# A 2-layer hybrid decoder step on one core: row products of the RWKV-7 chunk inverse moved to GpSimd, output weights split once and kept, group norm centred by a matmul

## The chip, the cores and the metric

One Trainium2 chip, one NeuronCore of it. TensorE (PE in the rows), VectorE (DVE), ScalarE (ACT) and GpSimd (POOL) each run their own instruction stream in order; SyncE (SP) only issues DMAs, also in order. The metric is the device time of one launch in microseconds, the median over runs.

## The reference, cut to what matters

Layer 0 (retention and RG-LRU) and both ConvFFNs are not touched. Layer 1 mixes time with RWKV-7: per head a 64x64 state, a per-head group norm of the result, and an output product.

```python
def rwkv7_step(S, inp):
    r_t, w_t, k_t, v_t, a_t, b_t = inp
    sa = jnp.einsum('bhij,bhj->bhi', S, a_t)
    S = S * w_t[:, :, None, :] + sa[..., None] * b_t[:, :, None, :] + v_t[..., None] * k_t[:, :, None, :]
    y = jnp.einsum('bhij,bhj->bhi', S, r_t)
    return S, y
...
    s_new, ys = lax.scan(rwkv7_step, s0, ...)          # 1040 prompt tokens, 16 heads of 64
    mu = jnp.mean(ys, axis=-1, keepdims=True)
    var = jnp.mean(jnp.square(ys - mu), axis=-1, keepdims=True)
    o = ((ys - mu) * lax.rsqrt(var + GN_EPS_C)).reshape(B, T, D) * p['gn_g'] + p['gn_b']
    bonus = jnp.sum(rh * kh * p['r_k'], axis=-1, keepdims=True) * vh
    o = (o + bonus.reshape(B, T, D)) * g
    return o @ p['w_o'], ...
```

All data are float32. The large products are done in three float32r passes: a weight block and its input are each split into a high and a low part.

## The kernel before, in words

The program runs layer 0, its FFN, Layer1A (all of RWKV-7 up to the recurrence; results go to scratch in DRAM), Layer1B (the recurrence and most of the output product), `finish` (the last quarter of the output product), and the second FFN. Instructions are emitted in the order in which they are to run: no scheduler reorders them.

**Layer1B.** The 1040 tokens are cut into 17 chunks of 64; a chunk's 16 heads are two halves, so there are 34 units (chunk, half). The string `UNIT = "pa z pt g1 u r r o r p2 g2 o o s o r y p3"` (L1641) is the order of work in one unit: `pa pt p2 p3` prepare the next unit (scores, transposes, the inverse's lower block), `z u s y` are the chain through the state, `g1 g2` the group norm of the previous unit, `r` takes one step of the inverse from a list, `o` one quarter of an output tile. So each unit has four `r` and four `o`. `s` ends with a copy of the new state on GpSimd (`s0v`, L1812), which stands once per unit in the trace and is used below as the unit's clock.

**The inverse (`inv_steps`, L1422).** For a group of four chunks, 128 blocks of 32x32 lie one per partition and I - A is inverted by forward substitution: row t takes a product of t x t elements (L1439, tile `pr`) and a sum over its rows (L1441, into column t of `mt`), both on VectorE; row t+1 reads column t. `CUTS` (L1636) puts rows 1 to 13 into three steps and each row from 14 to 31 into a step of its own. The first group is inverted in Layer1A; the other four (the last holds one chunk, on 32 partitions) in the recurrence, starting in units 0, 8, 16 and 24 and each to be done by the end of the sixth unit, when its results are loaded again from scratch. The block's input `at` is loaded in the first `r` of the same unit.

**Weights.** `load_next` (L270) loads blocks of 128x1024 (512 KB) two ahead on SP into two `wst` buffers. `split_next` (L279) makes `wh` on ScalarE and `wl` on VectorE (L323, L324), one block ahead, in two buffers each. The output weights `w_o`, eight blocks, are used four times, once for each block of about 260 tokens (`OBLK`), and loaded and split each time. The first three token blocks go beside the recurrence in the `o` slots, one output tile per unit in units 9 to 32; the last is `finish`.

**Group norm.** `gn_unit` (L1836): a matmul with the block of ones gives the sums (L1845), VectorE subtracts the mean (L1846), ScalarE squares (L1848). `gn_unit2`: a second matmul gives the variance (L1856), then ScalarE and VectorE make its inverse root (L1349 to L1352), and VectorE multiplies it in and applies the two gains (L1357, L1860, L1861); ScalarE and VectorE split the result (`yh`, `yl`).

Of the kernel before, what the change touches and what calls it, by code (L numbers as in the profile page):

```python
# [8 lines left out]
F32 = mybir.dt.float32  # L9
F32R = mybir.dt.float32r  # L10
AF = mybir.ActivationFunctionType
# [18 lines left out]
# ---------------------------------------------------------------- vectors  # L30
# [14 lines left out]
def constants():  # L45
    """Tables that depend on shapes alone."""
# [23 lines left out]
    m = np.zeros((128, 536), f)  # L70
# [9 lines left out]
    m[:, 408:536] = np.kron(np.eye(2), np.ones((64, 64)))  # L80
    c["masks"] = m
# [6 lines left out]
# ---------------------------------------------------------------- host layout  # L88
def cols(v):
    """(..., n*128) -> (128, ..., n): features on partitions."""  # L90
    v = np.asarray(v)
    r = v.reshape(v.shape[:-1] + (v.shape[-1] // 128, 128))
    return np.moveaxis(r, -1, 0)


def wblocks(w):
    """(K, M) -> (M/128, 128, K/128 * 128): one block per 128 output features."""
    k, m = w.shape
    return w.reshape(k // 128, 128, m // 128, 128).transpose(2, 1, 0, 3).reshape(m // 128, 128, k)


def gblocks(w, groups):
    """(K, 1024) cut along K in groups of g tiles -> blocks that hold 8, 4 or 2 output tiles x g K-tiles."""
# [89 lines left out]
# where the parts of a head pair's arithmetic stand beside the next products, in sixths of a 128-wide output tile  # L193
# [23 lines left out]
class Weave:  # L217
    """Emits dense steps and, between them, side steps as their share of the time comes up."""
# [43 lines left out]
class Prog:  # L262
# [6 lines left out]
    # ---- weights: loads two blocks ahead, exact split into two float32r parts one block ahead  # L269
    def load_next(self):  # L270
        if self.wq:
            w = self.wq.pop(0)
            src, pre = w if isinstance(w, tuple) else (w, None)
            n = src.shape[-1]
# [4 lines left out]
    def split_next(self):  # L279
        t, n, pre = self.loaded.pop(0)  # L280
        h = self.wsp.tile([128, 1024], F32R, tag="wh", name="wh")[:, :n]
        l = self.wsp.tile([128, 1024], F32R, tag="wl", name="wl")[:, :n]
        if pre is not None:
            self.scale_w(t, *pre)
        self.split(t, h, l)
        self.load_next()
        self.ready.append((h, l))
# [15 lines left out]
    def scale_w(self, t, kind, j):  # L303
        """Scales a block of w1 | a1 (or g1) by mix (j = 0) or 1 - mix along K."""
# [21 lines left out]
    # ---- one PSUM bank of a product: sum over k of W[k]^T X[k], in three exact float32r passes  # L326
# [21 lines left out]
    # steps of one 128-wide output tile, each token block in so many parts; evac(tb, psum view, c0, c1).  # L348
    # late: the weights of the next tile are not split before this one; pre: they are once its products are out
# [18 lines left out]
    # two tiles side by side at the start of a phase, each token block as soon as its norm is there  # L368
# [6 lines left out]
    # the same tile with the K-tiles outermost: each K-tile of X is done with as early as can be  # L375
# [15 lines left out]
    # steps of x += W^T y over a group of g K-tiles; a weight block holds 8/g output tiles  # L391
# [23 lines left out]
    # ---- RMS norm in parts: squares as the tiles of x become final, the scale per token block, then h  # L415
# [6 lines left out]
    # adds up squares over the features, all but the last few queued  # L422
# [8 lines left out]
    def rsqrt(self, y, v, t):  # L431
        """y = v ** -0.5: table value and one Newton step; t is scratch like v."""
# [17 lines left out]
    # emit(m, tb, rs) may return its second half, which then follows the next one's first  # L450
# [14 lines left out]
    # called after each step of the product that completes x: adds up the squares and queues the norm  # L465
# [36 lines left out]
class Layer0:  # L502
# [10 lines left out]
    # ---- retention, head h: q and k with the rotary applied (features on partitions), v by tokens  # L513
# [41 lines left out]
    def dense_ga(self, h, e):  # L555
        """Gate columns of head h: y = silu(g) * (normed o * gain), split as it comes."""
# [74 lines left out]
        # chunk 0: the sample rows, each with its own state, and the 16 leading prompt rows  # L631
# [68 lines left out]
        # the stages of a chunk are one step apart  # L700
# [8 lines left out]
    # ---- RG-LRU, one block of 128 features  # L709
# [21 lines left out]
    def lru_steps(self, g):  # L731
        """a = exp(-y) with y = 8 softplus(-lam) r, and sqrt(1 - a^2) = sqrt(t) (1 + a) with t = tanh(y / 2)."""
# [148 lines left out]
def softplus_neg(p, nc, pool):  # L881
    """lamc = 4 softplus(-lam) = 4 (max(-lam, 0) + ln(1 + exp(-|lam|)))."""
# [13 lines left out]
def layer0(p, pool, H, wv):  # L896
# [3 lines left out]
    # norm of the input: the squares of a token block beside the norm of the one before  # L900
# [25 lines left out]
    # the tensor engine's clock only rises with use  # L926
# [34 lines left out]
class FFN:  # L961
    """x += W_down^T (gelu(conv(W_ug^T h)) * (W_uv^T h)); f tiles are used in groups of four."""
# [1122 lines left out]
```

## Time and profile before

| what | value |
|---|---|
| runs (3) | 3524.53, 3528.8, 3534.92 us; median 3528.8 |
| profiled execution, first to last instruction | 3527.9 us |
| PE busy, DVE busy, ACT busy, POOL busy | 94%, 51%, 35%, 10% of the span |
| recurrence (units 0 to 33) | about 2218 to 2690 us of the span |
| `finish` and the norm after it | about 2690 to 2760 us |

No own time of the profiled execution stands beside its span, so sums are made against 3527.9 us; the median of the runs is 0.9 us above it. Busy shares over the whole span say little of the recurrence, which is 13% of it and has limits of its own: it is read by units and by windows.

### The profile page before, as it was taken

What the parts mean: (1) busy time and instruction counts of PE and PEld (TensorE: products, weight loads), DVE (VectorE), ACT (ScalarE), POOL (GpSimd) and SP (SyncE); (2) the same over time, 40 slices, a digit from 0 to 9 for tenths busy, and PEclk for the clock granted to TensorE, in tenths of its full rate; (3) what the DMA queues carried; (4) which work ended last, traced back from release to release, by engine and by line L of the source; (5) the groups of instructions that cost most, each with busy time, mean ns of one, the idle gap of its engine ahead of it and who ended that gap; (6) DMA issues with size and microseconds to landing.
All of it is one profiled execution on the core that took longest, in us unless ns stands there. A gap on an engine that the chain in (4) does not pass through costs nothing.

```text
span 3527.9 us, 55814 instructions
## 1 busy us (share of the span) xinstructions
PE 3305.9 (94%) x23480; PEld 3123.5 (89%) x23480; DVE 1800.3 (51%) x2860; ACT 1241.4 (35%) x2214; POOL 361.6 (10%) x650
## 2 busy tenths in 40 slices
PE   8999999998999999998978978788889999999998
PEld 7999999997999999997978878566767999999997
DVE  4444445556433333334765658677885533333334
ACT  4222224555322212123674444344445312212122
POOL 0110110000000000000111236111210000000000
PEclk9999999999999999999999989678999999999999
DMA  4111211111111111111356768845543111111111
GB/s 134 62 56 60 74 40 46 46 47 34 42 43 48 48 48 42 42 53 48 118 169 169 176 172 232 219 119 143 152 129 96 37 49 46 45 49 42 48 48 64
DMA packets 303066, 294.33 MB, mean 83 GB/s; under 512 B 233056, under 2 KB 248704, under 8 KB 300640
## 3 DMA queue, kind: packets, MB, share of 16 engines
q1 hardware_dynamic: 294368, 262.95, 25.6%
q0 software_dynamic: 8448, 27.82, 2.5%
q8 instruction: 185, 3.03, 0.4%
q14 instruction: 65, 0.53, 0.1%
HBM read 218.95 MB, written 67.47 MB: 81 GB/s over the span
## 4 chain that ended last, share of the span: by engine, by line
PE 29%; DVE 12%; DMA 4%; ACT 3%; issue 3%; SPq 1%; POOL 1%; DVEq 0%; POOLq 0%; ACTq 0%
PE d L337 8%; PE d L335 8%; PE d L336 8%; DVE pr L1439 2%; DVE mt L1441 1%; PE hs L1325 1%; DVE xsl L324 1%; DMA x<-d_pp 1%; DVE wl L324 1%; DMA kq<-d_kq 1%; PE nrm L429 1%; DMA at<-d_ab 1%; DVE x L1213 1%; DVE T L1439 0%; ACT x L1188 0%
## 5 line engine op out<-in xcount | busy, mean ns | idle before, releaser
L335 PE MATMUL d<-xsh,wh 128*128 128x350 f32 (+1 forms) x3656 | 1207.6, 330 | 11.5 <-ACT xsh L323 7.7
L337 PE MATMUL d<-xsl,wh 128*128 128x350 f32 (+1 forms) x3656 | 1193.6, 326 | 5.2 <-DVE xsl L324 5.1
L336 PE MATMUL d<-xsh,wl 128*128 128x350 f32 (+1 forms) x3656 | 1188.0, 325 | 4.4 <-DVE wl L324 4.4
L335 PEld LDWEIGHTS d<-xsh,wh 128*128 128x128 f32 x3656 | 696.2, 190 | 23.2 <-ACT xsh L323 9.3
L337 PEld LDWEIGHTS d<-xsl,wh 128*128 128x128 f32 x3656 | 694.6, 190 | 16.0 <-DVE xsl L324 14.7
L336 PEld LDWEIGHTS d<-xsh,wl 128*128 128x128 f32 x3656 | 696.9, 191 | 7.1 <-DVE wl L324 5.2
L335 PE MATMUL d<-T,wh 128*128 128x350 f32 (+1 forms) x1380 | 463.7, 336 | 15.8 <-DVE x L405 8.9
L324 DVE TENSOR_TENSOR wl<-wst,wh 128x1024 fp32r<-128x1024 f32 x248 | 303.1, 1223 | 320.3 <-ACT wh L323 320.3
L336 PE MATMUL d<-T,wl 128*128 128x350 f32 (+1 forms) x1380 | 445.2, 323 | 2.5 <-DVE wl L324 2.5
L337 PE MATMUL d<-T,wh 128*128 128x350 f32 (+1 forms) x1380 | 445.3, 323 | 1.4 <-DVE T L324 1.4
L323 ACT ACTIVATE wh<-wst 128x1024 fp32r<-128x1024 f32 x248 | 260.7, 1051 | 509.2 <-PE d L337 387.8
L405 DVE TENSOR_TENSOR x<-d,x 128x350 f32<-128x350 f32 (+1 forms) x450 | 230.3, 520 | 322.2 <-PE d L337 322.1
L991 DVE SCALAR_TENSOR_TENSOR T<-T,vec 128x1064 f32<-128x1064 f32 x88 | 116.8, 1327 | 398.2 <-ACT T L989 396.6
L335 PEld LDWEIGHTS d<-T,wh 128*128 128x128 f32 x1380 | 260.0, 188 | 28.2 <-DVE x L405 10.2
L336 PEld LDWEIGHTS d<-T,wl 128*128 128x128 f32 x1380 | 260.1, 188 | 9.9 <-DVE wl L324 3.2
L337 PEld LDWEIGHTS d<-T,wh 128*128 128x128 f32 x1380 | 260.2, 189 | 2.2 <-DVE T L324 2.2
L323 ACT ACTIVATE T<-T 128x1048 fp32r<-128x1048 f32 (+2 forms) x77 | 69.2, 899 | 288.1 <-DVE T L1004 241.2
L985 POOL TENSOR_SCALAR fcout<-T 128x2 f32<-128x2 f32 x44 | 11.2, 254 | 1515.1 <-ACT T L983 1515.1
L983 ACT ACTIVATE T<-d 128x350 f32<-128x350 f32 (+1 forms) x88 | 40.5, 461 | 269.6 <-PE d L337 269.6
L324 DVE TENSOR_TENSOR T<-T 128x1048 fp32r<-128x1048 f32 (+2 forms) x77 | 78.9, 1024 | 76.7 <-ACT T L323 76.7
L1004 DVE TENSOR_TENSOR T<-T,d 128x350 f32<-128x350 f32 x88 | 45.2, 515 | 120.5 <-PE d L337 120.4
L1439 DVE TENSOR_TENSOR pr<-mt,at 128x1 f32<-128x1 f32 (+45 forms) x124 | 93.9, 757 | 19.1 <-DMA at<-d_ab 13.5
(412 smaller groups left out, 4261.4 us busy)
## 6 DMA issues: line engine op xcount, KB each, us to landing
wst<-in_w_up SPq DMA_DIRECT2D x88, 512.0 KB, 3.2
wst<-in_w_down SPq DMA_DIRECT2D x44, 512.0 KB, 3.6
wst<-in_w_in SPq DMA_DIRECT2D x40, 512.0 KB, 3.2
kq<-d_kq SPq DMA_DIRECT2D x17, 1024.0 KB, 6.7
wst<-in_w_o SPq DMA_DIRECT2D x32, 512.0 KB, 4.0
T<-d_sv SPq DMA_DIRECT2D x80, 128.0 KB, 3.8
d_kq<-x SPq DMA_DIRECT2D x16, 544.0 KB, 4.4
d_kq<-x SPq DMA_DIRECT2D x32, 272.0 KB, 5.4
```

The lines of the kernel that those rows point to most:

```text
L323: self.nc.scalar.activation(out=h, in_=src, func=AF.Copy)
L324: (eng or self.nc.vector).tensor_tensor(out=l, in0=src, in1=h.bitcast(F32), op=OP.subtract)
L335: mm(ps, lhsT=h, rhs=a, start=start and j == 0, stop=False)
L336: mm(ps, lhsT=l, rhs=a, start=False, stop=False)
L337: mm(ps, lhsT=h, rhs=b, start=False, stop=stop and j == n - 1)
L405: self.nc.vector.tensor_tensor(out=xv, in0=ps, in1=xv, op=OP.add)
L429: self.nc.tensor.matmul(self.nps[tb][:, :n], lhsT=self.ones, rhs=sq, start=m == 0, stop=m == 7)
L983: nc.scalar.activation(out=ub[:, 18 + c0:18 + c1], in_=ps, func=AF.Copy)
L991: nc.vector.scalar_tensor_tensor(out=c, in0=ub[:, j:1064 + j], scalar=w[j], in1=c, op0=OP.mult, op1=OP.add)
L1004: nc.vector.tensor_tensor(out=st["f"][:, c0:c1], in0=c[:, 16 + c0:16 + c1], in1=ps, op=OP.mult)
L1213: nc.vector.tensor_tensor_scan(L, self.rst, s, 0.0, OP.mult, OP.add)
L1439: nc.vector.tensor_tensor(out=pr, in0=mt[:, 0:t, 0:t], in1=at[:, 0:t, t].unsqueeze(1).to_broadcast([n, t, t]), op=OP.mult)
```

## The change

Three edits. (1) From row 14 on, a row's product is issued to GpSimd right after the sum of the row before, and the `r` slot holds only the sum on VectorE. The lists start earlier: the first before the loop, the others in the unit before (units 7, 15, 23) with four empty slots behind the load. (2) At their first use the split parts of `w_o` are written to scratch (1 MB per block); the other three times `wh` and `wl` are loaded from there, with no split. (3) A third matrix, identity minus ones/64, takes the place of the ones in the first matmul of the group norm, so that the centred values stand in PSUM; ScalarE squares them from there, and VectorE's product with the inverse root reads them from there.

```diff
     def load_next(self):
             src, pre = w if isinstance(w, tuple) else (w, None)
+            if pre is not None and pre[0] == "again":
+                self.loaded.append((src, None, pre))
+                return
...
     def split_next(self):
+        again = pre is not None and pre[0] == "again"
...
+        if again:
+            for i, v in enumerate((h, l)):
+                self.nc.sync.dma_start(out=v.bitcast(F32), in_=t[i])
+        else:
...
+            self.split(t, h, l)
+            if pre is not None and pre[0] == "keep":
+                for i, v in enumerate((h, l)):
+                    self.nc.sync.dma_start(out=pre[1][i], in_=v.bitcast(F32))
...
-    def inv_steps(self, j, alloc, cuts, wait=0):
+    def inv_steps(self, j, alloc, cuts, wait=0, late=32):
...
+        def product(t):
+            at, mt = (st[k].rearrange("p (a b) -> p a b", b=32) for k in ("at", "mt"))
+            pr = st["pr"] = alloc("pr")[:n, :t * t].rearrange("p (c s) -> p c s", s=t)
+            nc.gpsimd.tensor_tensor(out=pr, in0=mt[:, 0:t, 0:t],
+                                    in1=at[:, 0:t, t].unsqueeze(1).to_broadcast([n, t, t]), op=OP.mult)
+
+        def total(t):
+            mt = st["mt"].rearrange("p (a b) -> p a b", b=32)
+            nc.vector.tensor_reduce(mt[:, 0:t, t], st["pr"], mybir.AxisListType.X, OP.add)
+            if t < 31:
+                product(t + 1)
+
+        def early(a, b):
+            rows(a, b)
+            if b == late < 32:
+                product(late)
...
-    return o + [io["w_o"][m] for _ in OBLK for m in range(8)]
+    return o + [(io["w_o"][m], ("keep", d["wo"][m])) if b == 0 else (d["wo"][m], ("again",))
+                for b in range(len(OBLK)) for m in range(8)]
-CUTS = [1, 8, 11] + list(range(14, 33))
+CUTS = [1, 8, 11, 14]
...
-        nc.tensor.matmul(py[:, 1], lhsT=p.bones, rhs=yf, start=True, stop=True)
-        nc.vector.scalar_tensor_tensor(out=yf, in0=py[:, 1], scalar=-1.0 / 64, in1=yf, op0=OP.mult, op1=OP.add)
+        nc.tensor.matmul(py[:, 1], lhsT=p.centre, rhs=yf, start=True, stop=True)
-        nc.scalar.activation(out=sq, in_=yf, func=AF.Square)
+        nc.scalar.activation(out=sq, in_=py[:, 1], func=AF.Square)
...
-        self.a.rs_mul(yf, v, y, sq)
+        self.a.rsq(v, y, sq)
+        nc.vector.tensor_tensor(out=yf, in0=py[:, 1], in1=sq, op=OP.mult)
...
-        inv = []
+        inv = self.a.inv_steps(1, alloc, CUTS, 0, CUTS[-1])
+        inv.pop(0)()
...
-            if c % 4 == 0 and f == 0 and c // 4 + 1 < 5:
-                inv = self.a.inv_steps(c // 4 + 1, alloc, CUTS, 1)
+            if i % 8 == 7 and c // 4 + 2 < 5:
+                inv += self.a.inv_steps(c // 4 + 2, alloc, CUTS, 4, CUTS[-1])
```

The instruction orders below are of the two built programs; line numbers of the changed one are its own.

VectorE in the third inverse before, from the last slot of unit 20 (row 28) through unit 21: products (`pr`), sums (`mt`), the masks of the next unit (`lz`, `ly`), the centring (`yf<-y,yf`) and the low part of a weight block (`wl`).

```order
L1883 TENSOR_TENSOR x<-d,x 128x256
L1439 TENSOR_TENSOR pr<-mt,at 128x784
L1441 TENSOR_REDUCE mt<-pr 128x28
L1718 TENSOR_TENSOR lz<-A,masks 64x4x64 x2
L1721 TENSOR_TENSOR ly<-A,masks 128x256 x2
L1846 SCALAR_TENSOR_TENSOR yf<-y,yf 128x256
L1439 TENSOR_TENSOR pr<-mt,at 128x841
L1441 TENSOR_REDUCE mt<-pr 128x29
L1439 TENSOR_TENSOR pr<-mt,at 128x900
L1441 TENSOR_REDUCE mt<-pr 128x30
L324 TENSOR_TENSOR wl<-wst,wh 128x1024
L1439 TENSOR_TENSOR pr<-mt,at 128x961
```

The same engine in the changed program, a unit earlier: from the last slot of unit 19 (row 25) through unit 20 to the group norm of the unit before.

```order
L1473 TENSOR_REDUCE mt<-pr 128x25
L1751 TENSOR_TENSOR lz<-A,masks 64x4x64 x2
L1754 TENSOR_TENSOR ly<-A,masks 128x256 x2
L1473 TENSOR_REDUCE mt<-pr 128x26
L1473 TENSOR_REDUCE mt<-pr 128x27
L1473 TENSOR_REDUCE mt<-pr 128x28
L1364 SCALAR_TENSOR_TENSOR sq<-sq,v 128x256
L1365 SCALAR_TENSOR_TENSOR sq<-sq,yr 128x256
L1891 TENSOR_TENSOR yf<-y,sq 128x256
L1893 TENSOR_TENSOR yf<-yf,gg 128x256
L1894 TENSOR_TENSOR yf<-yf,gg 128x256
```

Products, centring and `wl` are gone; the sums of three rows stand with nothing of VectorE between them, and each row comes one `r` slot earlier.

GpSimd in the changed program in the fourth inverse's like place (before, only the copies `s0v<-S` and the memset stood here).

```order
L1845 TENSOR_SCALAR s0v<-S 64x4x64 x2
L1468 TENSOR_TENSOR pr<-mt,at 128x676
L1717 MEMSET mt 32x8x32 x2
L1468 TENSOR_TENSOR pr<-mt,at 128x729
L1468 TENSOR_TENSOR pr<-mt,at 128x784
L1468 TENSOR_TENSOR pr<-mt,at 128x841
L1845 TENSOR_SCALAR s0v<-S 64x4x64 x2
```

Four products stand between one unit's state copy and the next's, the first right behind the copy.

SP at the end of the recurrence and in `finish`, before:

```order
L276 DMA wst<-in_w_o 128x1024
L1695 DMA gg<-d_gg 128x1024
L276 DMA wst<-in_w_o 128x1024 x2
L1807 DMA out_rwkv_p<-S 128x256 x2
L276 DMA wst<-in_w_o 128x1024 x5
L276 DMA wst<-in_w_up 128x1024 x10
```

and in the changed program, the last two weight blocks of `finish`:

```order
L291 DMA wh<-d_wo 128x1024
L291 DMA wl<-d_wo 128x1024
L280 DMA wst<-in_w_up 128x1024
L291 DMA wh<-d_wo 128x1024
L291 DMA wl<-d_wo 128x1024
L280 DMA wst<-in_w_up 128x1024 x9
```

Each block is two loads, straight into the buffers that the matmuls read, where before it was one load into a staging buffer two blocks ahead.

## Rows read from the trace of the kernel before

**Rows 1.** Timeline of POOL: start, length (us), line, operation; state copies of units 7 to 31.

```profile
2330.60 1.77 POOL L1812 TENSOR_SCALAR s0v<-S 64x256 f32<-64x256 f32 x2 [10.21 <-DVE S L1804]
...
2443.25 1.77 POOL L1812 TENSOR_SCALAR s0v<-S 64x256 f32<-64x256 f32 x2 [9.75 <-DVE S L1804]
...
2459.87 1.82 POOL L1812 TENSOR_SCALAR s0v<-S 64x256 f32<-64x256 f32 x2 [12.39 <-DVE S L1804]
2472.96 1.77 POOL L1812 TENSOR_SCALAR s0v<-S 64x256 f32<-64x256 f32 x2 [11.27 <-DVE S L1804]
...
2485.09 2.51 POOL L1812 TENSOR_SCALAR s0v<-S 64x256 f32<-64x256 f32 x2 [9.64 <-PE Tp L1733]
2498.57 2.14 POOL L1812 TENSOR_SCALAR s0v<-S 64x256 f32<-64x256 f32 x2 [10.97 <-DVE S L1804]
...
2514.47 3.21 POOL L1812 TENSOR_SCALAR s0v<-S 64x256 f32<-64x256 f32 x2 [13.04 <-PE Tp L1733]
2532.45 2.48 POOL L1812 TENSOR_SCALAR s0v<-S 64x256 f32<-64x256 f32 x2 [14.77 <-DVE S L1804]
...
2544.06 1.78 POOL L1812 TENSOR_SCALAR s0v<-S 64x256 f32<-64x256 f32 x2 [7.24 <-PE Tp L1757]
2555.60 1.77 POOL L1812 TENSOR_SCALAR s0v<-S 64x256 f32<-64x256 f32 x2 [9.76 <-DVE S L1804]
...
2666.66 1.77 POOL L1812 TENSOR_SCALAR s0v<-S 64x256 f32<-64x256 f32 x2 [10.96 <-DVE S L1804]
```

**Rows 2.** Timeline of DVE in unit 21, the longest of the third inverse.

```profile
2514.49 1.55 DVE L1439 TENSOR_TENSOR pr<-mt,at 128x784 f32<-128x784 f32 x1
...
2517.08 0.86 DVE L1718 TENSOR_TENSOR lz<-A,masks 64x256 f32<-64x256 f32 x2
...
2518.52 0.41 DVE L1846 SCALAR_TENSOR_TENSOR yf<-y,yf 128x256 f32<-128x256 f32 x1
...
2524.38 1.22 DVE L324 TENSOR_TENSOR wl<-wst,wh 128x1024 fp32r<-128x1024 f32 x1
...
2527.35 1.16 DVE L1441 TENSOR_REDUCE mt<-pr 128x31 f32<-128x961 f32 x1
2528.42 0.41 DVE L1351 SCALAR_TENSOR_TENSOR sq<-sq,v 128x256 f32<-128x256 f32 x1
...
2532.28 0.42 DVE L1883 TENSOR_TENSOR x<-d,x 128x256 f32<-128x256 f32 x1
```

**Rows 3.** Waits, 2215 to 2690 us: who waited for whom, us, times, longest.

```profile
ACT yh L323 <- DVE yf L1861: 144.1, 34, 10.2
...
DVE pr L1439 <- DMA at<-d_ab: 13.5, 3, 8.1
```

**Rows 4.** POOL multiplies and subtracts of two tensors: timeline rows, and one operation's shortest/median/longest (ns).

```profile
2178.76 1.26 POOL L1520 TENSOR_TENSOR T<-T 128x512 f32<-128x512 f32 x1 [3.75 <-DMA T<-d_sv]
2179.98 1.03 POOL L1521 TENSOR_TENSOR T<-T,sa 128x512 f32<-128x512 f32 x1
```

```profile
L324 POOL TENSOR_TENSOR xsl<-T,xsh x6: 2397/2774/3482, 1721.0 to 2028.1; 128x1048 fp32r<-128x1048 f32 x6
```

**Rows 5.** Timelines of DVE and POOL at 2161 us, where both worked.

```profile
2161.90 2.46 DVE L1439 TENSOR_TENSOR T<-x 128x784 f32<-128x784 f32 x1
```

```profile
2160.74 2.14 POOL L1521 TENSOR_TENSOR T<-T,sa 128x512 f32<-128x512 f32 x1
```

**Rows 6.** `finish`: two of VectorE's adds, one per output tile; DMA issues (count, KB, median us to landing).

```profile
2705.70 0.44 DVE L1883 TENSOR_TENSOR x<-d,x 128x272 f32<-128x272 f32 x1 [1.28 <-PE d L337]
...
2709.30 0.44 DVE L1883 TENSOR_TENSOR x<-d,x 128x272 f32<-128x272 f32 x1 [1.28 <-PE d L337]
```

```profile
kq<-d_kq SPq DMA_DIRECT2D x17, 1024.0 KB, 6.7
wst<-in_w_o SPq DMA_DIRECT2D x29, 512.0 KB, 3.3
```

**Rows 7.** Window: its length, busy us of PE, PEld, DVE, ACT, POOL; granted clock, DMA share, GB/s.

```profile
2235.00:2260.00 25.00, 20.30 (x308) 15.43 (x308) 20.08 (x51) 11.76 (x35) 4.31 (x6) 0.77 1.00 315
```

More of the change, by code (lines that the diff above doesn't have):

```diff
@@ L69, in constants @@
     c["ctab"] = ct.astype(f)
-    m = np.zeros((128, 536), f)
+    m = np.zeros((128, 664), f)
     m[:, 0:128] = np.eye(128)
@@ L80, in constants @@
     m[:, 408:536] = np.kron(np.eye(2), np.ones((64, 64)))
+    m[:, 536:664] = np.eye(128) - m[:, 408:536] / 64
     c["masks"] = m
@@ L280, in split_next @@
         t, n, pre = self.loaded.pop(0)
+        again = pre is not None and pre[0] == "again"
+        n = 1024 if again else n
         h = self.wsp.tile([128, 1024], F32R, tag="wh", name="wh")[:, :n]
         l = self.wsp.tile([128, 1024], F32R, tag="wl", name="wl")[:, :n]
-        if pre is not None:
-            self.scale_w(t, *pre)
-        self.split(t, h, l)
+        if again:
+            for i, v in enumerate((h, l)):
+                self.nc.sync.dma_start(out=v.bitcast(F32), in_=t[i])
+        else:
+            if pre is not None and pre[0] != "keep":
+                self.scale_w(t, *pre)
+            self.split(t, h, l)
+            if pre is not None and pre[0] == "keep":
+                for i, v in enumerate((h, l)):
+                    self.nc.sync.dma_start(out=pre[1][i], in_=v.bitcast(F32))
         self.load_next()
@@ L1449, in out @@
             nc.gpsimd.dma_start(out=flat(d["mm"][4 * j:min(4 * j + 4, NCH)]), in_=tt)
-        return [load] + [lambda: None] * wait + [lambda a=a, b=b: rows(a, b) for a, b in zip(cuts[:-1], cuts[1:])] + [out]
+        def product(t):
[12 more added lines that the diff above has]
+                product(late)
+        return ([load] + [lambda: None] * wait + [lambda a=a, b=b: early(a, b) for a, b in zip(cuts[:-1], cuts[1:])] +
+                [lambda t=t: total(t) for t in range(late, 32)] + [out])
     def samp_pre(self):
@@ L1629, in run, with w_order_l1 @@
             f()
-def w_order_l1(io):
+def w_order_l1(io, d):
     l1 = io["w_lora1"]
@@ L1967, in build @@
         xt = p.x = const.tile([128, 8, T], F32, name="x")
-        masks = const.tile([128, 536], F32, name="masks")
+        masks = const.tile([128, 664], F32, name="masks")
         p.ones = const.tile([128, 128], F32, name="ones")
@@ L1971, in build @@
         p.ident, p.causal, p.mask0 = masks[:, 0:128], masks[:, 128:256], masks[:24, 256:280]
-        p.rwmask, p.bones = masks[:, 280:408], masks[:, 408:536]
+        p.rwmask, p.bones, p.centre = masks[:, 280:408], masks[:, 408:536], masks[:, 536:664]
         with tc.manual_schedule():
-            p.wq += w_order_l0(io) + w_order_ffn(io, 0) + w_order_l1(io) + w_order_ffn(io, 1)
+            d = scratch(pool)
+            p.wq += w_order_l0(io) + w_order_ffn(io, 0) + w_order_l1(io, d) + w_order_ffn(io, 1)
             c0, c1 = TBS[0]
@@ L1983, in build @@
             nc.vector.memset(p.ones, 1.0)
-            d = scratch(pool)
             p.keep = pool("keep")
@@ L2055, in scratch @@
               "ab": [NCH, 16, 2, 32, 32], "mt": [NCH, 16, 2, 32, 32], "mm": [NCH, 16, 2, 32, 32], "sv": [5, 16, NS, 64]}
-    return {n: dr.tile(sh, F32, name="d_" + n) for n, sh in shapes.items()}
+    t = {n: dr.tile(sh, F32, name="d_" + n) for n, sh in shapes.items()}
+    t["wo"] = dr.tile([8, 2, 128, 1024], F32, name="d_wo")
+    return t
 def ffn_phase(p, H, l, wv, pool, cost, emit):
```

## The prediction

> **What bounds the kernel now.** Read three views in this order: POOL's timeline for its state copies, which fall once in a unit and so time the 34 units; VectorE's timeline inside a long unit; and the list of waits, for who is late. The copies [rows 1] show that units are not alike. In the third inverse (units 16 to 23) they take 16.6, 13.1, 12.1, 13.5, 15.9, 18.0, 11.6 and 11.5 us, 112.4 in all. The last two hold no row of an inverse; about 11.5 us is what a unit costs when VectorE is free, and TensorE sets that. So the six units with rows lie some 20 us above it in each group of eight. The second group (2330.60 to 2443.25) is 112.7 us, the fourth (2555.60 to 2666.66) 111.1 [rows 1].
>
> Inside the longest unit VectorE has no gap [rows 2]: 1.55 us of product, 1.16 of sum, 1.22 of `wl` follow each other, and ScalarE waits for it up to 10.2 us with `yh` [rows 3]; behind `yh` stands the copy on which TensorE's next transposes depend. So in these units VectorE's own length is the unit's length. The first unit of a group is long for another reason: VectorE waits for `at` just loaded, up to 8.1 us [rows 3].
>
> **What the change removes.** Four inverses have 18 products each from row 14 on, with 9,597 elements per partition. VectorE's rate there is 1.55 us for 784 elements, 1.98 ns each [rows 2], so 19 us per inverse leave it. `wl` (1.22 us) leaves 16 units and the eight tiles of `finish`, and ScalarE's part with it; the centring (0.41) leaves all 34 units. In a unit without rows these gain next to nothing: TensorE's 11.5 us cover them; I count 0.3 us there.
>
> **What it adds on the path: the products again, on another engine.** Row t+1 needs column t, so VectorE's sum, GpSimd's product and the next sum are a chain, and VectorE stands still while GpSimd multiplies, unless something of its own lies between. The order of the changed program shows two places where something does: `lz` and `ly`, which take 2517.08 to 2518.52, 1.45 us [rows 2], and the block from the group norm to the add of an output tile, 2528.42 to about 2532.6, 4.2 us [rows 2]. Between the other three sums of a unit nothing lies.
>
> Does the 4.2 us block hide a product? Where both engines worked on tensors in SBUF, they took turns [rows 5]: VectorE's product of 784 elements, 1.55 us elsewhere, took 2.46, because it started at 2161.90 and GpSimd's held until 2162.88; the state copies, 1.77 us alone, took 3.21 beside a product of VectorE's [rows 1]. Five of the block's instructions read two SBUF tensors. GpSimd is waiting when the first of them ends, and so I take the product as not hidden there.
>
> The price of a product on GpSimd is not in the trace. The nearest rows [rows 4]: two plain operands, 1.26 us for 512 elements and 2.397 for 1048, so 2.12 ns each and 0.17 fixed; one operand repeated within a row, 1.03 for 512, so 1.67 ns. The product repeats an operand too, but reads it with a stride of 32 elements. VectorE pays for that stride 1.98 ns against 1.19 (`wl`, 1.22 us for 1024) [rows 2], 1.66 times; applied to GpSimd's 2.12 that is 3.5. Bounds 1.67 and 3.5; I take 2.4, near their geometric mean, since the repeat and the stride pull in opposite directions. With the fixed 0.17 doubled for the two handovers between the engines, a product costs 0.35 us + 2.4 ns per element: 0.9 at row 15, 1.7 at row 24, 2.7 at row 31.
>
> The Trainium skill (GPSIMD Engine Reference, section 7, Performance pitfalls for Q7 kernels) puts a read whose step is over 8 bytes at about 2.9 cycles per element in place of 1.9; by that extra cycle at its 1.2 GHz I would estimate 2.9 ns. No row of this trace has such a read on GpSimd.
>
> **The sum for the third inverse.** A sum costs 1.16 us for 961 elements, 1.2 ns each [rows 2]. Per unit: four sums + the two or three products in the open + 4.2 + the product behind the fourth sum, which starts about 0.5 us late behind the state copy (1.77 us, issued before it) and hides `lz` and `ly`.
> - unit 17 (rows 14 to 17): 1.2 + 2.9 + 4.2 + 1.6 = 9.9, so TensorE's 11.4 hold
> - unit 18 (18 to 21): 1.8 + 3.9 + 4.2 + 2.0 = 12.0
> - unit 19 (22 to 25): 2.7 + 5.2 + 4.2 + 2.5 = 14.5
> - unit 20 (26 to 29): 3.6 + 6.7 + 4.2 + 3.0 = 17.5
> - unit 21 (30, 31 and the transposed copy, about a sum long): 2.2 + 1.1 + 2.7 + 4.2 + 1.5 = 11.7
> - unit 16 (rows 1 to 13, no wait for `at`, which is now loaded a unit earlier): about 7 of rows + 1.5 + 4.2 = 12.7
>
> Together 79.8 against 89.2 now, and 0.6 for the two free units: 10 us gained. The gain is the wait for `at` (4) and the last unit, where two rows fewer stand (6); units 18 to 20 lose a little, as a product costs there as much as the VectorE work that left.
>
> The other inverses by the same sums: the second keeps `wl` in units 9 to 16, since there the weights are split and kept, five times 1.2 us, so 4 gained; the fourth has 32 partitions, a shorter load and a first unit of less wait, 7; the first has no `wl` and no output tiles before it and was partly held by loads, 2. Recurrence: 23 us gained.
>
> **What the weights cost elsewhere.** At the start DMA is full: share 1.00 at 315 GB/s from 2235 to 2260 us [rows 7]. The first kept block is written just before, 1 MB, 3.3 us at that rate, on SP ahead of the recurrence's first loads: 3 lost, 6 at most, 0 if hidden. In the recurrence a block now moves 1 MB per unit of 11 to 18 us and is asked for a unit ahead: nothing, covered by a whole unit of matmuls.
>
> In `finish` that cover is gone. An output tile takes 2705.70 to 2709.30, 3.6 us [rows 6]. A block's buffer comes free when the tile before the last ends, so its two loads have one tile's time. One 512 KB load lands in 3.3 us, one of 1 MB in 6.7 [rows 6]; two together I take at 5.0. Of eight tiles six wait 1.4 us: 8 lost (0 if both land within 3.6, 19 at 6.7).
>
> Sum: -23 + 3 + 8 = -12 on the span of 3527.9, 3516; against the median 3517.
>
> **Rivals.**
> - *Cheap products.* GpSimd reads the repeated column at 1.67 ns and does not hold up the 4.2 us block. Then units 17 to 21 fall to TensorE's 11.4: third inverse 20 us gained, second 15, fourth 18, first 14, so -67 + 11, 3473. With the turns kept it is less: the four inverses hold 4 x 9,597 elements, 38 us per ns; 0.73 ns below my price are 28 us, less 2 that TensorE's floor keeps, so 49 gained, 3491. For it: GpSimd's own row for a repeated operand. Against it: the stride, and the turns in rows 5.
> - *The stride costs GpSimd what it costs VectorE.* At 3.5 ns the products cost 1.1 x 38 = 42 us more than in the forecast, so +19 in the recurrence, with 11 elsewhere +30: 3559, slower. It decides from about 2.7 ns per element, where the recurrence's gain equals the 11 lost. For it: VectorE's own 1.66 [rows 2]. Against it: GpSimd reads the repeated operand faster than a plain one [rows 4]. By the 2.9 of the Trainium skill's page (GPSIMD Engine Reference, section 7) the kernel would be at about 3536, this rival's near end.
> - *Nothing moves.* The recurrence gains only the wait for `at` (about 11 over three inverses) and `finish` and the start take that back: 3528. For it: in the middle units a product's price is close to what left VectorE.
>
> **How the numbers follow.** Chances: forecast (3503 to 3524) 0.36, cheap products (3470 to 3503) 0.27, nothing moves (3524 to 3540) 0.17, dear stride 0.20. Low bound of the unknowns: 49 gained and nothing lost elsewhere, 3480; high: +19, 6 and 19, 3573. Eight in ten: 3482 to 3556. A measurement of this kernel can tell about 0.3%, 11 us (3518 to 3539). Faster takes the cheap case and a little over half of the forecast's, 0.47; the same the rest of that and most of the third, 0.29; slower 0.24.
>
> **What would show it.** In POOL's timeline: `pr` of 961 elements at 2.5 us (1.8 or 3.5 for the rivals). In the state copies: unit 20 near 17.5 us, unit 21 near 12, unit 16 near 13. In VectorE's waits: `mt` for POOL's `pr`, some 25 us per inverse, the largest new entry. The wait of `pr` for `at` gone. In `finish`: adds 5 us apart, TensorE waiting for the loads of `wl`. I am wrong if the products are hidden behind VectorE's group norm, or if `finish` keeps 3.6 us per tile.

## The result, and the profile after

The changed kernel is slower: 3557.9 us median against 3527.8, ratio 1.0085 with a 95% interval of 1.007 to 1.010. The forecast was 3517 with a range of 3482 to 3556, so the time lies outside it. The profiled execution of the changed kernel took 3554.1 us, its span is 3552.3 us, 24.4 us longer than that of before.

Where are they? The state copies on POOL's timeline answer to [rows 1]; from the first copy (unit 0) to the last (unit 31) it is 443.2 us now and was 430.7. Units 1 to 7 and 8 to 15 are together 8.4 and 8.5 us longer (103.1 and 121.1 for 94.7 and 112.7), units 16 to 23 and 24 to 31 shorter by 0.6 and 3.8. The third group after (start, length, line, operation; idle time before it and its releaser):

```profile
2462.87 1.78 POOL L1845 TENSOR_SCALAR s0v<-S 64x256 f32<-64x256 f32 x2 [9.07 <-DVE S L1837]
2475.06 1.77 POOL L1845 TENSOR_SCALAR s0v<-S 64x256 f32<-64x256 f32 x2 [9.69 <-PE y L1859]
...
2501.17 1.77 POOL L1845 TENSOR_SCALAR s0v<-S 64x256 f32<-64x256 f32 x2 [3.58 <-DMA wh<-d_wo]
2515.68 1.77 POOL L1845 TENSOR_SCALAR s0v<-S 64x256 f32<-64x256 f32 x2 [3.52 <-DVE S L1837]
2534.68 1.77 POOL L1845 TENSOR_SCALAR s0v<-S 64x256 f32<-64x256 f32 x2 [3.58 <-DVE S L1837]
2550.17 1.77 POOL L1845 TENSOR_SCALAR s0v<-S 64x256 f32<-64x256 f32 x2 [3.21 <-DVE S L1837]
2563.98 1.77 POOL L1845 TENSOR_SCALAR s0v<-S 64x256 f32<-64x256 f32 x2 [11.31 <-PE Tp L1790]
2574.63 1.78 POOL L1845 TENSOR_SCALAR s0v<-S 64x256 f32<-64x256 f32 x2 [7.08 <-DVE S L1837]
```

Unit 16 takes 12.2 us (16.6 before), the longest is now unit 20 with 19.0 (unit 21 before, 18.0), and unit 22, which has no row, takes 13.8 (11.6). The list of waits over 2235 to 2700 us says who is late (us, times, longest):

```profile
ACT yh L336 <- DVE yf L1894: 130.0, 33, 8.7
...
PEld y L1856 <- issue: 85.6, 33, 9.2
PE y L1856 <- DVE yf L1891: 79.9, 27, 9.1
DVE lz L1751 <- ACT a L1748: 60.4, 23, 4.1
DVE mt L1473 <- POOL pr L1468: 60.1, 37, 2.9
```

The wait for `at` of [rows 3] is gone. VectorE's `mt` for POOL's `pr` was foreseen. TensorE's first matmul of `y` waiting for VectorE's `yf` (79.9 us) was not; no such row stands in the list of before. `yf` at L1891 is the group norm's product, which since the change reads the centred values out of `py`. Before, the same matmul (there L1823) waited 1.9 us in all, for ScalarE, and TensorE's long waits stood at other places (list of before, same window):

```profile
PE Tp L1733 <- ACT mt L1760: 37.4, 18, 8.0
PE y L1856 <- ACT sq L1848: 31.7, 20, 2.9
...
PE y L1823 <- ACT v L1857: 1.9, 5, 0.4
```

The two long ones are gone in the changed kernel, so the 79.9 us are not all added time. Unit 20, a selection of rows by engine (it belongs to the third inverse; the order of GpSimd that the section on the change gives for the fourth is this unit's):

```profile
2522.10 2.11 POOL L1468 TENSOR_TENSOR pr<-mt,at 128x729 f32<-128x729 f32 x1 [1.91 <-DVE mt L1473]
...
2524.24 0.92 DVE L1473 TENSOR_REDUCE mt<-pr 128x27 f32<-128x729 f32 x1 [2.29 <-POOL pr L1468]
...
2527.53 0.97 DVE L1473 TENSOR_REDUCE mt<-pr 128x28 f32<-128x784 f32 x1 [2.38 <-POOL pr L1468]
...
2528.59 2.52 POOL L1468 TENSOR_TENSOR pr<-mt,at 128x841 f32<-128x841 f32 x1 [1.08 <-DVE mt L1473]
2528.87 2.51 DVE L1365 SCALAR_TENSOR_TENSOR sq<-sq,yr 128x256 f32<-128x256 f32 x1
2531.49 0.42 DVE L1891 TENSOR_TENSOR yf<-y,sq 128x256 f32<-128x256 f32 x1
...
2532.06 0.37 PE L1856 MATMUL y<-kq,s0v 64*64 64x64 f32 x4 [4.67 <-DVE yf L1891]
```

Read it downwards. VectorE stands still 2.29 and 2.38 us for products. Then a step of the group norm, `sq`, takes 2.51 us instead of 0.42, until GpSimd's product beside it is through. Only then comes the product that reads `py`, and 0.15 us after its end TensorE may write the next unit's `py`: it stood for 4.67 us with everything behind it in its queue.

### The profile page after: what moved, and what is told of

The parts are those of the page before. It is cut to its first block, busy times and chain, and to the rows that moved or that the text cites. A ratio compares the mean times of both kernels' runs of the same rounds, so it can differ in the third digit from the quotient of the medians.

```text
span 3552.3 us, 55881 instructions
## 1 busy us (share of the span) xinstructions
PE 3317.5 (93%) x23480; PEld 3133.1 (88%) x23480; DVE 1700.6 (48%) x2730; ACT 1227.5 (35%) x2190; POOL 468.6 (13%) x722
## 4 chain that ended last, share of the span: by engine, by line
PE 33%; DVE 9%; ACT 3%; DMA 3%; POOL 2%; issue 2%; SPq 1%; DVEq 0%; POOLq 0%; ACTq 0%
PE d L348 8%; PE d L350 8%; PE d L349 8%; POOL pr L1468 2%; PE A L1742 1%; PE y L1856 1%; PE hs L1338 1%; PE y L1859 1%; DVE sq L1365 1%; DVE mt L1473 1%; DMA x<-d_pp 1%; DVE xsl L337 1%; DVE x L1226 1%; PE nrm L442 0%; DMA kq<-d_kq 0%
## 5 line engine op out<-in xcount | busy, mean ns | idle before, releaser
L348 PE MATMUL d<-xsh,wh 128*128 128x350 f32 (+1 forms) x3656 | 1205.8, 330 | 11.9 <-ACT xsh L336 7.7
L350 PEld LDWEIGHTS d<-xsl,wh 128*128 128x128 f32 x3656 | 693.7, 190 | 15.6 <-DVE xsl L337 14.5
L337 DVE TENSOR_TENSOR wl<-wst,wh 128x1024 fp32r<-128x1024 f32 x224 | 273.9, 1223 | 303.1 <-ACT wh L336 303.1
L336 ACT ACTIVATE wh<-wst 128x1024 fp32r<-128x1024 f32 x224 | 235.2, 1050 | 508.1 <-PE d L350 389.4
L1856 PE MATMUL y<-kq,s0v 64*64 64x64 f32 x544 | 52.7, 277 | 80.4 <-DVE yf L1891 79.9
L1468 POOL TENSOR_TENSOR pr<-mt,at 128x196 f32<-128x196 f32 (+17 forms) x72 | 118.9, 1651 | 65.6 <-DVE mt L1473 54.2
L1856 PEld LDWEIGHTS y<-kq,s0v 64*64 64x64 f32 x544 | 32.3, 157 | 94.5 <-issue 85.6
```

The source lines that it names most:

```text
L336: self.nc.scalar.activation(out=h, in_=src, func=AF.Copy)
L337: (eng or self.nc.vector).tensor_tensor(out=l, in0=src, in1=h.bitcast(F32), op=OP.subtract)
L348: mm(ps, lhsT=h, rhs=a, start=start and j == 0, stop=False)
L350: mm(ps, lhsT=h, rhs=b, start=False, stop=stop and j == n - 1)
L1468: nc.gpsimd.tensor_tensor(out=pr, in0=mt[:, 0:t, 0:t], in1=at[:, 0:t, t].unsqueeze(1).to_broadcast([n, t, t]), op=OP.mult)
L1856: nc.tensor.matmul(py[r, m, :], lhsT=t["s0v"][r, g, h, :], rhs=t["kq"][r, g, 3, :], start=True, stop=False)
```

## The experiments

Three theories were set up. T1: the centring by a matmul holds the only PSUM buffer of `py` until VectorE has read it, and that is the loss. T2: the products on GpSimd are. T3: the kept weights are. Times are medians, each beside before's on the same chip; differences are to that.

### The three edits, one at a time

The centring alone, on the kernel before:

```diff
-        nc.tensor.matmul(py[:, 1], lhsT=p.bones, rhs=yf, start=True, stop=True)
-        nc.vector.scalar_tensor_tensor(out=yf, in0=py[:, 1], scalar=-1.0 / 64, in1=yf, op0=OP.mult, op1=OP.add)
+        nc.tensor.matmul(py[:, 1], lhsT=p.centre, rhs=yf, start=True, stop=True)
...
-        self.a.rs_mul(yf, v, y, sq)
+        self.a.rsq(v, y, sq)
+        nc.vector.tensor_tensor(out=yf, in0=py[:, 1], in1=sq, op=OP.mult)
```

> The kernel before with the centring by a matmul alone: rows and output weights stay as before. T1 (the centred values stay in the unit's one PSUM buffer until VectorE has read them, so TensorE's next y step waits for VectorE): slower by 12 to 30 us, 3540 to 3558 us, and a wait of y's first matmul on VectorE's product, some 50 us or more in all, which the kernel before doesn't have. T2 (the products on GpSimd are what costs): 3523 to 3532 us. T3 (the kept weights cost it): the same as T2.

Measured: 3557.3 us, +31.8, ratio 1.0087 (1.0068 to 1.0107). The recurrence (first to last state copy) takes 461.3 us, 30.6 more than before. The wait is there in 31 units (list of waits, 2235 to 2700 us):

```profile
PEld y L1824 <- issue: 90.2, 31, 7.3
PE y L1824 <- DVE yf L1859: 85.3, 31, 7.2
```

How do 85.3 us of waiting make 30.6 us of loss? The windows of the whole recurrence, first before, then this run (length; busy us of PE, PEld, DVE, ACT, POOL; granted clock, DMA share, GB/s):

```profile
2235.90:2666.70 430.80, 356.40 (x4934) 288.11 (x4936) 344.78 (x686) 195.79 (x523) 82.92 (x110) 0.85 0.53 144
```

```profile
2234.40:2695.70 461.30, 374.97 (x4916) 303.75 (x4914) 334.33 (x655) 205.47 (x520) 82.55 (x110) 0.80 0.50 135
```

TensorE stands still 86.3 us, where before it was 74.4 in other places: 11.9 more. The larger part, 18.6 us, is TensorE's busy time, for nearly the same number of matmuls (4916 and 4934 records) at a mean granted clock of 0.80 for 0.85, so more of it at the lower level of 1.2 GHz. The hold seems to cost more through the clock than through the standing; no run takes the two apart.

The kept weights alone:

```diff
+            for i, v in enumerate((h, l)):
+                self.nc.sync.dma_start(out=v.bitcast(F32), in_=t[i])
...
-    return o + [io["w_o"][m] for _ in OBLK for m in range(8)]
+    return o + [(io["w_o"][m], ("keep", d["wo"][m])) if b == 0 else (d["wo"][m], ("again",))
+                for b in range(len(OBLK)) for m in range(8)]
```

> The kernel before with the kept weights alone. By the profile of the changed kernel 2.7 us later at the first state copy and 5.6 us more over the eight adds of the last output block: 3534 to 3538 us under T1 and T2, which both leave this as it is. T3 (the weights are the main loss, since their transfers and lacking splits also shift the recurrence): 3545 us or more.

Measured: 3536.4 us, +10.9, ratio 1.0032 (1.002 to 1.0044). Its profiled execution took 3526.2 us, 10 less than this median, so it shows where time moves but not the whole loss. In it the first state copy comes 9.8 us earlier than before, the recurrence gains 3.7 us, the time from the last state copy to the first add of `finish` grows by 3.4, `finish` from its first to its last add by 4.4 (28.8 for 24.4).

The products and the early load alone:

```diff
+            nc.gpsimd.tensor_tensor(out=pr, in0=mt[:, 0:t, 0:t],
+                                    in1=at[:, 0:t, t].unsqueeze(1).to_broadcast([n, t, t]), op=OP.mult)
...
+        inv = self.a.inv_steps(1, alloc, CUTS, 0, CUTS[-1])
+        inv.pop(0)()
```

> The kernel before with the early load of the inverse's block and the products of rows 14 to 31 on GpSimd, centring and weights as before. T1: the recurrence gains what the changed kernel shows in units 16 to 31 and doesn't lose what it shows in units 1 to 15, so 3510 to 3524 us. T2: slower by 8 to 25 us, 3536 to 3553 us. T3: 3520 to 3530 us.

Measured: 3513.9 us, -11.6, ratio 0.9966 (0.9954 to 0.9978). Together: 31.8 + 10.9 - 11.6 = 31.1, and the whole change measures 30.0. The edits add up, and T1 names the one that costs most.

### Is it the buffer, or the centring itself?

A PSUM tile of their own for the centred values does not fit beside the others (18 KB per partition in all; the run e4_own_psum has no time). So in the changed kernel they go to 256 columns of the `T` buffer that nothing used:

```diff
-        nc.tensor.matmul(py[:, 1], lhsT=p.centre, rhs=yf, start=True, stop=True)
+        w["ce"] = self.pT[:, :, 384:512]
+        for i in range(2):
+            nc.tensor.matmul(w["ce"][:, i], lhsT=p.centre, rhs=yf[:, i * 128:i * 128 + 128], start=True, stop=True)
```

> The changed kernel, with the centred values in 256 columns of the buffer of the transposed factors that nothing used (two matmuls of 128 columns in place of one of 256): y's buffer is free again after ScalarE's reading of the variance. T1 (the hold of y's buffer costs): the wait of y's first matmul on VectorE's product, 79.9 us before, is gone and 22 to 35 us come back: 3522 to 3536 us. Rival T1b (not the buffer but the centring's own chain costs: a dearer matmul, ScalarE's square and VectorE's product reading PSUM): 3550 to 3560 us, with the wait gone or moved.

Measured: 3526.8 us, +1.8, ratio 1.0012 (0.9996 to 1.0029). Beside the changed kernel's +30.0, 28 us came back, with the same centring arithmetic. The same without kept weights:

```diff
-    return o + [(io["w_o"][m], ("keep", d["wo"][m])) if b == 0 else (d["wo"][m], ("again",))
-                for b in range(len(OBLK)) for m in range(8)]
+    return o + [io["w_o"][m] for _ in OBLK for m in range(8)]
```

> The same, with the output weights loaded and split as before the change, so that it is the products on GpSimd with a centring that holds nothing. If the three edits add up and the centring without its hold is worth nothing: as the products alone, 3510 to 3517 us. If the shorter chain that the centring was to give is worth something: 3498 to 3508 us. T1b: 3535 us or more.

Measured: 3522.2 us, -2.8, ratio 0.9994 (0.9978 to 1.001): 9 us short of the products alone, and in none of the ranges. The waits show that the hold had in part moved. `prep3` writes other columns of the same bank, and now it waits for VectorE's reading:

```profile
PEld Tp L1777 <- DVE yf L1881: 46.9, 21, 7.9
PE Tp L1777 <- DVE yf L1881: 44.0, 21, 7.8
...
PE Tp L1867 <- ACT bk L1755: 24.1, 32, 1.0
```

The second new wait (L1867) is the centring matmul's own, for ScalarE's reading of the same buffer. In the products-only run neither stands; there TensorE waits 41.5 us at another `Tp` matmul and 13.3 at `y`. That makes 13 us more waiting here, which is near the missing 9; the two profiles suggest it and do not prove it.

So a third form, on the early-load kernel described below, lets ScalarE copy the centred values to SBUF, so that VectorE reads no PSUM there:

```diff
-        nc.tensor.matmul(py[:, 1], lhsT=p.bones, rhs=yf, start=True, stop=True)
-        nc.vector.scalar_tensor_tensor(out=yf, in0=py[:, 1], scalar=-1.0 / 64, in1=yf, op0=OP.mult, op1=OP.add)
+        nc.tensor.matmul(py[:, 1], lhsT=p.centre, rhs=yf, start=True, stop=True)
...
+        nc.scalar.activation(out=yf, in_=py[:, 1], func=AF.Copy)
```

> The early-load kernel with the centring by a matmul, its result copied to SBUF by ScalarE (0.38 us a unit more there, 0.41 us a unit less on VectorE): no hold of a PSUM buffer by VectorE anywhere. T1 in full (only the hold costs): 3492 to 3502 us, no wait of y's first matmul on VectorE's product. T1b (a centring by matmul costs in itself, as the 8 us between the products-only run and the run with spare columns could say): 3506 us or more.

Measured: 3497.8 us, -26.9, ratio 0.9918 (0.99 to 0.9936); early load alone is at -25.2. The wait of `y` for VectorE is gone, and in the profile the recurrence takes 393.7 us where early load alone takes 402.8. So this is in T1's range: centring by a matmul costs nothing that shows; reading its result late did.

### What GpSimd's products cost

The early load alone, with products and sums on VectorE as before:

```diff
-            if c % 4 == 0 and f == 0 and c // 4 + 1 < 5:
-                inv = self.a.inv_steps(c // 4 + 1, alloc, CUTS, 1)
+            if i % 8 == 7 and c // 4 + 2 < 5:
+                inv += self.a.inv_steps(c // 4 + 2, alloc, CUTS, 4)
```

> The kernel before with the inverse's block loaded early alone; products and sums stay on VectorE. If the 11.6 us that the products with the early load gained are GpSimd's doing: 3522 to 3527 us here (the rows' wait for the load was 13.5 us in all, of which little lies on the path). If they are the load's: 3512 to 3517 us.

Measured: 3499.8 us, -25.2, ratio 0.9924 (0.9902 to 0.9946). Outside both ranges: the load is worth twice what products and load together gain, so moving the products lost some 14 us. Unit 16 is 12.2 us, as in the changed kernel. The products' price and what stands beside it, from the products-only run (groups by line and shape: count, busy us, mean ns, idle before):

```profile
L1455 POOL TENSOR_TENSOR pr<-mt,at 128x961 f32<-128x961 f32 x3 | 8.2, 2721 | 2.5 <-DVE mt L1460 2.4
...
L1455 POOL TENSOR_TENSOR pr<-mt,at 128x196 f32<-128x196 f32 x3 | 2.1, 712 | 8.9 <-issue 8.5 <-POOL s0v L1832 0.4
```

```profile
L1460 DVE TENSOR_REDUCE mt<-pr 128x14 f32<-128x196 f32 (+17 forms) x72 | 50.6, 703 | 68.0 <-POOL pr L1455 68.0
L1352 DVE SCALAR_TENSOR_TENSOR sq<-sq,yr 128x256 f32<-128x256 f32 x31 | 32.1, 1034 | 1.1
```

(2721 - 712) / (961 - 196) = 2.63 ns per element and 0.2 us fixed. VectorE idles 68.0 us for the products, and `sq` takes 1034 ns in the mean, 425 in the kernel before. Is that the chain of product and sum, or the engines in each other's way? Two runs. The first sets the places for a sum apart (on the spare-column kernel without kept weights):

```diff
-UNIT = "pa z pt g1 u r r o r p2 g2 o o s o r y p3"
+UNIT = "pa r z pt g1 u r o p2 r g2 o o s o r y p3"
```

> The run with the spare columns and no kept weights, and in each unit the four places at which a row's sum is asked for spread apart (no two next to each other), so that a product on GpSimd has time before its sum. If what was left of GpSimd's price is VectorE standing at the sum for a product that just began (68 us over 44 waits in the products-only run): 8 to 15 us faster than the run without it, some 3495 to 3505 us. If GpSimd's share of VectorE's time or order elsewhere decides: within 4 us of it.

Measured: 3523.1 us, -1.9, ratio 1.000 (0.9985 to 1.0016), 0.9 from the run without it; VectorE's wait for products is 78.7 us for 79.4. A product starts only when the sum before it is through; spreading the sums did not change that wait, so this run does not decide. The second lets GpSimd compute products that nothing reads, beside VectorE's own rows:

```diff
+                if t >= 14 and j:
+                    p2 = alloc("p2")[:n, :t * t].rearrange("p (c s) -> p c s", s=t)
+                    nc.gpsimd.tensor_tensor(out=p2, in0=at[:, 0:t, 0:t],
+                                            in1=at[:, 0:t, t].unsqueeze(1).to_broadcast([n, t, t]), op=OP.mult)
```

> The early-load kernel, in which GpSimd also computes a product of each row from 14 on, that nothing reads and that waits for nothing but the block's load; VectorE still does all rows itself. If the 14 us that products on GpSimd lost against early load alone are the two engines slowing each other at SBUF (in the products-only run one VectorE step on SBUF took 2.53 us for 0.43 while a product ran): 8 to 25 us slower than early load alone, 3508 to 3525 us, with VectorE's rows and SBUF steps longer. If they are the series product, sum, product: 3497 to 3503 us.

Measured: 3550.2 us, +25.5, ratio 1.0075 (1.0062 to 1.0088), so 51 us above early load alone, twice the most that was expected, with no dependency of a row on GpSimd. Its timelines of DVE and POOL in one long unit:

```profile
2513.27 8.86 POOL L1440 TENSOR_TENSOR p<-at 128x676 f32<-128x676 f32 x3
...
2517.09 0.92 DVE L1445 TENSOR_REDUCE mt<-pr 128x27 f32<-128x729 f32 x1
2517.92 2.18 DVE L324 TENSOR_TENSOR wl<-wst,wh 128x1024 fp32r<-128x1024 f32 x1
2520.02 3.45 DVE L1443 TENSOR_TENSOR pr<-mt,at 128x784 f32<-128x784 f32 x1
2523.51 0.97 DVE L1445 TENSOR_REDUCE mt<-pr 128x28 f32<-128x784 f32 x1
...
2528.50 2.59 POOL L1816 TENSOR_SCALAR s0v<-S 64x256 f32<-64x256 f32 x2 [6.37 <-DVE S L1808]
```

VectorE's steps with two SBUF operands wait their turn: `wl` 2.18 us for 1.22 and the product of 784 elements 3.45 for 1.55 [rows 2]. A sum, which has one operand, is not longer: that of 729 elements takes 0.92 beside a product, and 914 ns in the mean in the kernel before. Nor did the state copy queue behind the extra products: GpSimd had been idle for 6.37 us when it began, and at least 3.1 us in every other unit. The Trainium skill (SBUF — State Buffer, section SBUF: two separate sides) states that a VectorE step with two SBUF inputs and a GpSimd step that reads SBUF exclude each other for their whole length; the trace agrees. That the exclusion costs is shown. Its 51 us are no measure of the 14, since here VectorE's own products meet GpSimd's as well; how the 14 us divide between exclusion and the chain of sums and products is not shown.

Which products lose? Only rows 14 to 20 on GpSimd:

```diff
-            if t < 31:
+            if t < 20:
                 product(t + 1)
```

> The early load with only the products of rows 14 to 20 on GpSimd; rows 21 to 31 are VectorE's whole. If the 14 us lost by all 72 products go with GpSimd's time (short rows have about a quarter of it): 3500 to 3506 us. If each handing over costs alike, whatever its size: 28 of 72 rows, 3504 to 3509 us. If short products hide and only the long ones hurt: below 3497 us.

Measured: 3502.2 us, -22.5, ratio 0.9933 (0.9913 to 0.9952), 2.7 us behind early load alone. That fits a loss in proportion to GpSimd's time; it is within what two medians can tell apart, but no gain from short rows shows.

### Where the kept weights lose

On the early-load kernel, weights kept for blocks 1 and 2 alone, and then only written:

```diff
-    return o + [io["w_o"][m] for _ in OBLK for m in range(8)]
+    return o + [(io["w_o"][m], ("keep", d["wo"][m])) if b == 0 else (d["wo"][m], ("again",)) if b < 3 else io["w_o"][m]
+                for b in range(len(OBLK)) for m in range(8)]
```

> The early-load kernel with the split weights kept for blocks 1 and 2 alone; the last block's are loaded and split as before. T3 as the bookkeeping has it (the start loses 2.7 us, the recurrence gains some 4, the last block loses 5 to 8): with the last block left out, 3494 to 3500 us. If the keeping costs in the recurrence too: 3502 to 3510 us.

Measured: 3511.0 us, -13.7, ratio 0.9957 (0.9943 to 0.997), 11.5 behind early load alone and 1 us beyond the dearer of the two ranges.

```diff
-    return o + [io["w_o"][m] for _ in OBLK for m in range(8)]
+    return o + [(io["w_o"][m], ("keep", d["wo"][m])) if b == 0 else io["w_o"][m]
+                for b in range(len(OBLK)) for m in range(8)]
```

> The early-load kernel, in which the first block's split weights are written to scratch and never read: all four blocks are loaded and split as before the change. If the 11 us that keeping weights for blocks 1 and 2 cost are the writes': 3506 to 3514 us. If they are the rereads' (two loads into buffers that TensorE still reads, at the moment of need): 3497 to 3503 us.

Measured: 3502.9 us, -21.9, ratio 0.9939 (0.9921 to 0.9957). By the medians the writes cost some 3 us and the rereads the larger part. One unit of the run with blocks 1 and 2 kept shows a late reread (SP's issues, then TensorE):

```profile
2527.39 0.62 SPq L1703 DMA_DIRECT2D uv<-d_vt  x1
...
2528.06 0.63 SPq L290 DMA_DIRECT2D wh<-d_wo  x1
...
2533.62 0.29 PEld L347 LDWEIGHTS d<-yh,wh 128*128 128x128 f32 x1 [5.57 <-issue]
2533.65 0.55 PE L347 MATMUL d<-yh,wh 128*128 128x256 f32 x1 [5.46 <-DMA wh<-d_wo]
```

The reload stands on SP behind the loads of a chunk, which are issued at the end of a unit. It lands late, TensorE stands for 5.46 us, and unit 23 takes 17.9 us where early load alone has 10.2. In that profile the recurrence as a whole is no longer than with early load alone (402.1 and 402.8 us): most other units of the last two groups are about 1 us shorter, and make up for TensorE's waits for reloads, 10.6 us in all. In these two profiles the difference stands ahead of any reread, at the first state copy (2243.0 and 2231.1 us), and the first copies of all profiles scatter from 2226 to 2245 us. So that the rereads cost some 8 us rests on the medians; where they lose it is not shown.

### A version that beats both

Rows on VectorE, loaded a unit earlier and dealt out over eight units (numbers are steps, `-` an empty place), first alone:

```diff
+LATER = "L - - 0 1 2 3 4 5 6 7 8 9 10 11 - 12 13 14 - 15 16 - - 17 18 - - 19 20 O -"
...
-            if i % 8 == 7 and c // 4 + 2 < 5:
-                inv += self.a.inv_steps(c // 4 + 2, alloc, CUTS, 4)
+            if i % 8 == 6 and c // 4 + 2 < 5:
+                inv += self.place(c // 4 + 2, alloc, LATER)
```

> The early-load kernel with the same rows on VectorE, dealt out over the units: blocks 2 to 4 are loaded a unit earlier and their rows stand in eight units, the long ones two or three to a unit where four stood. If VectorE's load in the two longest units (15.6 and 15.7 us busy of 16.5 each) sets their length while the two units without rows are TensorE's at 10.2 to 10.5 us: 15 to 30 us faster than early load alone, 3470 to 3485 us. If the length of the long units comes from the chain of steps whatever VectorE has to do: within 5 us of 3500 us.

Measured: 3497.2 us, -27.5, ratio 0.992 (0.9905 to 0.9936). The median gains 2 us on early load alone, the recurrence in the profile 8.7 (394.1 us); the expected 15 to 30 did not come. The longest unit of the third inverse fell from 16.5 to 14.0, but unit 23 rose from 10.2 to 15.1. With ScalarE's copy of the centred values added:

```diff
-        nc.vector.scalar_tensor_tensor(out=yf, in0=py[:, 1], scalar=-1.0 / 64, in1=yf, op0=OP.mult, op1=OP.add)
+        nc.scalar.activation(out=yf, in_=py[:, 1], func=AF.Copy)
```

> Rows on VectorE, loaded early and dealt out evenly, with the centring by a matmul and ScalarE's copy. In the profiles each of the two gained some 9 to 10 us on the stretch from the last layer stage to the end of the last block over early load alone, though only 2 to 3 us in the medians. If the gains of the stretch are real and add up: 3480 to 3490 us. If the medians are right: 3492 to 3498 us.

Measured: 3481.4 us, -43.3, ratio 0.9874 (0.9855 to 0.9894), the fastest of all; the recurrence takes 380.5 us, 50 less than before. 402.8 less 8.7 less 9.1 would be 385.0, and the median is 18 us below early load alone: the two gains seen in the profiles add up. That each alone moved the median by only 2 us fits the later first state copies in their profiles, 5.4 and 9.5 us behind early load alone's; why those came later is open.

## Why the prediction was wrong, step by step

- **The centring: the step that failed.** "In a unit without rows these gain next to nothing" counted the 0.41 us that leave VectorE. It did not ask who reads `py` last. Before, that was ScalarE with `v`; now it is VectorE's product, which stands in VectorE's queue behind the rows' sums, the weights' split and the waits for GpSimd. `psb` has one buffer per name, so TensorE's next `y` waits. Price: 31.8 us alone and 28 in the changed kernel, against nothing in the sum.
- **The recurrence's 23 us: too large, and near by luck where it was near.** The run with the spare columns has all three edits without the hold of `y`; in its profile the recurrence gains 11.9 us (418.8). Units 16 to 20 take 11.5, 12.1, 12.5, 14.5 and 17.4 us there, forecast 12.7, 11.4, 12.0, 14.5 and 17.5. Two errors nearly cancel in that. A unit's last sum falls behind the state copy, so a unit counted by copies holds a row earlier than I summed, about 0.8 us less in unit 20; and a product costs 2.63 ns per element, not 2.4, about 0.7 us more there. Unit 21 gets what was put off, row 29's sum and row 30's product, and takes 14.7 for 11.7. Unit 23 takes 16.4, with a late reload. The rule of the Trainium skill (GPSIMD Engine Reference, section 7, Performance pitfalls for Q7 kernels) led to an estimate of 2.9; the measurement lies between. The repeated, strided operand does cost GpSimd, less than the stride costs VectorE, and the rival that decides from 2.7 ns was not reached.
- **How the 23 were made up was wrong too.** The early load alone is worth 25. Of its part in the third inverse, the wait for `at` was right (4; unit 16 fell by 4.4), and two rows fewer in unit 21 were not (6; with the rows on VectorE it fell by 1.5). The gain in units 1 to 15 (16.9 of 27.9 us in its profile; I counted 6 for them, weights and centring included) was missed. The products were taken as nearly neutral in the third inverse; moving them loses 14 in all.
- **Turns at SBUF: right.** The product is not hidden behind the group norm: in unit 20 `sq` stands 2.51 us for it. In the changed kernel unit 20 took 19.0 us, unit 16 12.2 and unit 21 15.5. VectorE's wait for products was to be some 25 us per inverse and the largest new entry; it is 60.1 over the four, less than the wait of `y`.
- **Weights, start 3 and `finish` 8: near in sum (10.9 measured), not shown term by term.** From its first to its last add `finish` lost 5.6 us in the changed kernel and 4.4 with the kept weights alone, with the wait for the reloads that was forecast; 3.0 and 3.4 more stand just ahead of it. The 3 at the start cannot be read from the profiles: the first state copy came 2.7 us later in the one and 9.8 earlier in the other. "Nothing" in the recurrence did not look at SP's queue, where a reload behind a chunk's loads came late. The row of that wait in `finish` (after, 2690 to 2745 us):

```profile
PEld d L349 <- DMA wl<-d_wo: 4.5, 4, 1.6
```

- **The rival on the slower side** gave 3559, 1 us from the time, by luck: it needed 3.5 ns per element. None of the rivals held the buffer.

## What to carry to other kernels

When an edit changes which engine reads a PSUM tile last, look up how many buffers the tile has and who writes it next; the instruction saved is the small part. Before a product moves to GpSimd, count VectorE's steps with two SBUF operands that will meet it, and whether the next sum has to wait for it: here the two together took back more than VectorE gained. A load and its rows started earlier were worth more than any arithmetic moved: try the cheap edit alone before the bundle.

## What was not expected of the hardware

The units without rows became shorter although nothing in them changed. Windows of units 22 and 23 (length; busy us of PE, PEld, DVE, ACT, POOL; granted clock), first before, then early load alone:

```profile
2532.45:2544.06 11.61, 11.61 (x132) 9.43 (x132) 7.93 (x17) 5.83 (x14) 4.14 (x7) 0.73 0.47 141
2544.06:2555.60 11.54, 11.54 (x184) 9.62 (x182) 6.55 (x16) 7.02 (x20) 1.70 (x3) 1.00 0.61 181
```

```profile
2507.58:2518.11 10.53, 10.29 (x160) 8.48 (x161) 6.85 (x16) 6.49 (x18) 2.31 (x4) 1.00 0.56 160
2518.11:2528.36 10.25, 10.25 (x160) 8.52 (x160) 6.56 (x16) 6.28 (x16) 3.34 (x5) 1.00 0.83 235
```

In the first of the two TensorE works with hardly a gap in both kernels (11.61 of 11.61 us, 10.29 of 10.53), but before at a mean granted clock of 0.73, so partly at its lower level of 1.2 GHz, after a unit in which it had been busy 13.09 of 17.98 us; with the early load it was busy 12.24 of 16.55 us in the unit ahead and kept 1.00. Unit 23 ran at 1.00 in both, but before it still had the matmuls that unit 22 left over (184 records for 160); the two units together have 316 and 320. The 11.5 us that the prediction took for TensorE's own floor was thus not one: it is nearer 10.3. No run took the clock apart from the order of the work.
